# Output rows of six tiles from VectorE to ScalarE and GpSimd, squares to ScalarE, and a fourth slot between softmax and product with V, in a hybrid attention layer

## The chip, the core and the metric

The kernel runs on one core of one Trainium2 chip. Its engines work in parallel, each through its own list of instructions in order: PE (TensorE, matrix products), ACT (ScalarE), DVE (VectorE), POOL (GpSimd), and SP (SyncE), which here only issues transfers. PEld is PE's weight load. Semaphores make one engine wait for another. The metric is the device time of one execution in microseconds (us); the number given for a kernel is the median of several executions.

## The reference

One layer over 1024 tokens of 1024 columns. A joint projection feeds two groups of heads: group A is grouped-query attention with rotary positions, group B is attention over a neighbourhood of 8 x 16 tokens on a grid 64 wide. Both are gated, joined, projected, and added to x; a last RMSNorm follows.

```
h = _rmsnorm(x, norm_gain[l])
proj = h @ w_in[l]
q_a, k_a, v_a, g_a, q_b, k_b, v_b, g_b = jnp.split(proj, split_at, axis=-1)
... # RMSNorm and axial rotary positions of q_a and k_a
o_a = _gqa_blocked(q_a, k_a, v_a) * jax.nn.silu(g_a)
o_b = _neighbourhood_attn(q_b, k_b, v_b, na_rpb[l]) * jax.nn.silu(g_b)   # softmax(q k / 8 + bias) v, masked
mixed = jnp.concatenate([o_a, o_b], axis=-1)
x = x + mixed @ w_out[l]
return _rmsnorm(x, final_norm_gain)
```

The change bears on the neighbourhood attention (group B), on `mixed @ w_out`, and on the addition of x.

## The kernel before

The 1024 tokens are eight tiles of 128 rows (u = 0..7). Weights come in groups g of 256 columns: 0 to 12 are the joint projection, 13 to 16 the output projection. Each weight and each input of a projection is split into two fp16 numbers, a high part made by ACT (for weights L414, for a tile's mixed rows L933) and a low part made by DVE from the high one (L419, L937). A product of one tile with one group is 24 matmuls (eight chunks of the contraction by high-high, high-low, low-high), all recorded at line L504.

The span falls into four stages: projections (to about 160 us), attention A (160 to 360), attention B (364 to 506), and the rest of the output projections (506 to 549).

**Attention B** goes through 32 *pairs*: a tile u, taken in the order 0, 7, 1, 2, 3, 4, 5, 6, and two of its eight heads. For one pair PE makes the scores (L833, L836). DVE adds the bias and takes the row maximum (`b_qk`, L854, one instruction a head); ACT makes two exponentials (L856) and converts them to fp16 as the high part (L858); DVE makes the low part (`b_lo`, L863); a transposing transfer on SP's queue turns both (L865) into one of three buffers (`ptb`); PE multiplies them with V (L883 to L885). After every second pair DVE evacuates the product (L892 to L895) and POOL multiplies it into the gated rows `mixB` (L897).

**The mixed rows of a tile** are prepared for the output projection by `os_start`: the mean square (ACT the first half, L920; DVE the second, L925, which adds to the first), a scaling (L927), POOL's power -1/2 (L928), two high parts by ACT (L933), two low parts by DVE (L937), and two transposing transfers (L946).

**Output rows.** `out_gen` makes two products (256 columns each) into one PSUM bank, a *job*: of one tile and two groups, or of the first two tiles and one group. `add` on DVE then scales the rows and adds x, one instruction a product (L994), into a buffer loaded with x before. `fin_a` squares the finished half rows on ACT (L1019), and `fin_b` makes the last norm (L1025 to L1030).

**The order of the work.** `run_units` goes through slots i = 0, 1, ... In slot i the program is emitted in this order: some due jobs of ACT, the low part of pair i-1, the scores and softmax of pair i, more jobs of ACT, jobs of DVE, then 4.2 chunks (six matmuls each) of *filler* on PE, then the product with V of pair i-3 (`SKEW_B`). Filler is a queue of generators: gate projections (g = 11, 12) first, then output jobs. Work for ACT and DVE that isn't the softmax is put into a list with a cost (`job("dve", 0.5 * len(jobs), add, late=0)`), and `Flow.work` takes jobs from it in each slot until an allowance in microseconds is spent. So a change of costs or engines moves other jobs to other slots too. [...]

Of the kernel before, what the change touches and what calls it, by code (L numbers as in the profile page):

```python
# [8 lines left out]
F32 = mybir.dt.float32  # L9
F16 = mybir.dt.float16  # L10
BF16 = mybir.dt.bfloat16
AF = mybir.ActivationFunctionType
OP = mybir.AluOpType
# [3 lines left out]
P = 128  # L17
KC = 8
NU = 8
GC = 256  # L20
# [2 lines left out]
NX = 4  # L23
BASE_A, BASE_B = (1.72, 2.6, 2.8), (1.7, 1.6, 2.0)
HAND = 6
SKEW_A, SKEW_B = 5, 3
FILL_A = [(4, 5.0), (7, 4.2)]
FILL_A_END = 3.6
CHUNKS_A = 264
# [10 lines left out]
SLOTS = {"both": (16384, 2048, 4), "qc": (24576, 2048, 2), "stg1": (28672, 2048, 3), "stg": (18432, 2048, 3),  # L40
         "t": (0, 3072, 3), "ptb": (9216, 3072, 3), "th": (32896, 2048, 1), "y": (32896, 2048, 1),
         "p32": (AREA + 14464, 3072, 1)}
ORDER = (0, 7, 1, 2, 3, 4, 5, 6)
# [4 lines left out]
class Flow:  # L48
# [17 lines left out]
    def job(self, eng, cost, fn, *a, delay=1, late=1, key=None):  # L66

        self.jobs.append((late, self.slot + delay, self.number(), eng, cost, fn, a, key, self.tail))
# [83 lines left out]
def kernel(ctx: ExitStack, tc: tile.TileContext, x: bass.AP, w: bass.AP, wo: bass.AP,  # L152
# [3 lines left out]
    act, dve, pool, pe, sp = nc.scalar, nc.vector, nc.gpsimd, nc.tensor, nc.sync  # L156
# [3 lines left out]
    whl = ctx.enter_context(tc.tile_pool(name="whl", bufs=2))  # L160
# [7 lines left out]
    at, job = fl.at, fl.job  # L168
# [22 lines left out]
    def area(off, shape, dt):  # L191
        return carve(ar, off + 16384, shape, dt)

    turn = {}

    def slot(kind, shape, dt):

        off, size, n = SLOTS[kind]
        k = turn[kind] = turn.get(kind, -1) + 1
        off += k % n * size  # L200
        return area(off, shape[1:], dt) if off < AREA else carve(rq, off - AREA, shape[1:], dt)
# [13 lines left out]
    raw, wp, late, x2 = {}, {}, {}, {}  # L215
# [24 lines left out]
    for c in range(2):  # L240
        cs = slice(c * 512, (c + 1) * 512)
# [566 lines left out]
    def keys(u):  # L808

        a = max(u - 1, 0)  # L810
        return a, min(u + 1, NU - 1) - a + 1
# [49 lines left out]
    def b_lo(u, p):  # L861
        hl, p32 = hls.pop(("b", u, p))
        dve.scalar_tensor_tensor(hl[:, 1], p32, 2.0 ** 14, hl[:, 0], op0=OP.mult, op1=OP.subtract)  # L863
        pt = slot("ptb", [P, 4 * keys(u)[1], P], F16)
        sp.dma_start_transpose(pt, hl.rearrange("p a k -> p (a k)"))  # L865
        pts["b", u, p] = pt

    def b_pv(u, p):
        pt = pts.pop(("b", u, p))
        n = keys(u)[1]  # L870
        for e in range(2):
            b_pv_head(u, 2 * p + e, pt[:, e * n:e * n + n], pt[:, (2 + e) * n:(3 + e) * n])
# [29 lines left out]
    mT, rws, osp = {}, {}, {}  # L902
# [4 lines left out]
    def os_start(u):  # L907

        if not all({("b", u, c), ("a", u // 2, c * GC)} <= ready for c in range(2)):
            at(1, "post", os_start, u)  # L910
            return
        t = rws[u] = tn(f"os{u}", 4, "os")
        k = ORDER.index(u)
        hl = one.tile([P, 2, 1024], F16, tag=f"q{k % 2}0" if k > 3 else "gain", name=f"mhl{u}")
        osp[u] = [hl[:, 0], hl[:, 1]]
        ms = mixed(u)
        cs = [slice(i * 512, (i + 1) * 512) for i in range(2)]

        def sq():
            act.activation(late["r"][0][:, 2048:2560].bitcast(BF16), ms[0], AF.Square, accum_out=t[:, 0:1])  # L920
            job("dve", 0.95, scale, delay=0, late=0, key=("os", u))

        def scale():
            junk = late["r"][1][:, 2048:2560] if k else osp[u][0][:, cs[1]]
            dve.tensor_tensor_reduce(out=junk.bitcast(BF16), in0=ms[1], in1=ms[1], scale=1.0, scalar=t[:, 0:1],  # L925
                                     op0=OP.mult, op1=OP.add, accum_out=t[:, 1:2])
            dve.tensor_scalar(t[:, 1:2], t[:, 1:2], 2.0 ** -30, 1e-36, op0=OP.mult, op1=OP.add)  # L927
            pool.tensor_tensor(t[:, 2:3], t[:, 1:2], mh[:, :1], op=OP.pow)  # L928
            for i in range(2):
                job("act", 0.72, hi, i, delay=1, late=0, key=("os", u))  # L930

        def hi(i):
            act.activation(osp[u][0][:, cs[i]], ms[i], AF.Copy, scale=t[:, 2:3])  # L933
            job("dve", 0.8, lo, i, delay=0, late=0, key=("os", u))

        def lo(i):
            dve.scalar_tensor_tensor(osp[u][1][:, cs[i]], ms[i], t[:, 2:3], osp[u][0][:, cs[i]], op0=OP.mult, op1=OP.subtract)  # L937
            if i:
                dve.reciprocal(t[:, 3:4], t[:, 2:3])
                os_c(u)  # L940
        job("act", 0.82, sq, delay=1, late=0, key=("os", u))

    def os_c(u):
        mT[u] = [m.bitcast(F16).rearrange("p (a b) -> p a b", b=P) for m in mixed(u)]
# [36 lines left out]
    def load_x2(u):  # L981
        if u not in loaded:
            loaded.add(u)
            sp.dma_start(x2[u], rows_of(x, u, 1024, 0, 1024))

    def out_gen(jobs, done=()):

        pt = proj_tile(f"po{jobs[0][0]}_{jobs[0][1]}")
        rw = tn(f"rw{jobs[0][0]}_{jobs[0][1]}", 2, "rw")
        def add():  # L990
            for i, (u, g) in enumerate(jobs):
                cs = slice((g - 13) * GC, (g - 12) * GC)
                load_x2(u)
                dve.scalar_tensor_tensor(x2[u][:, cs], pt[:, i], rw[:, i:i + 1], x2[u][:, cs], op0=OP.mult, op1=OP.add)  # L994
        def then():
            job("dve", 0.5 * len(jobs), add, late=0)
            for u, h in done:
                job("act", 0.82, fin_a, u, h, delay=2, late=2)

        for i, (u, g) in enumerate(jobs):  # L1000
            need_w(g)
            fl.need(("os", u), lambda: u in mT)
            if i == 0 and jobs[-1] == (u, g + 1) and g + 1 in ready:
                dve.tensor_tensor(rw, col(RC + g, 2), rws[u][:, 3:4].to_broadcast([P, 2]), op=OP.mult)
            elif i == 0 or not both:
                dve.tensor_tensor(rw[:, i:i + 1], rws[u][:, 3:4], col(RC + g), op=OP.mult)
            both = i == 0 and jobs[-1] == (u, g + 1) and g + 1 in ready
            hi, lo = wp[g]
            seq = [(mT[u][a][:, k], b[:, k]) for k in range(KC) for a, b in ((0, hi), (0, lo), (1, hi))]
            yield from chunks([((pt[:, i], l, r), dict(start=n == 0, stop=n == 23))  # L1010
                               for n, (l, r) in enumerate(seq)], 6, then if i == len(jobs) - 1 else None)
# [185 lines left out]
    a, b = ORDER[2:4]  # L1197
# [7 lines left out]
    def hooks2(i):  # L1205
        hooks(i)
        for u, k in zip(ORDER, SPLIT_AT):
            if i - SKEW_B == k:
                at(0, "post", os_start, u)

    for u in ORDER[4:7]:
# [3 lines left out]
    def parts_b(i, back):  # L1215
        def first():
            if 1 <= i <= 32:
                b_lo(*ub[i - 1])
            if i < 32:
                b_qk(*ub[i])  # L1220
        return first, None, (lambda: b_pv(*ub[i - back])) if i >= back else None

    with run_units(32, SKEW_B, parts_b, rates(FILL_B, FILL_B_END), hooks2):
        pass
# [93 lines left out]
```

## Time and profile before

| | us |
|---|---|
| median of 3 runs (lowest to highest) | 556.71 (555.53 to 557.19) |
| the profiled execution's own time | 558.52 |
| its span, first to last instruction | 556.7 |
| PE busy (92% of the span) | 511.8 |
| DVE busy (81%) | 448.4 |
| ACT busy (67%) | 373.5 |
| POOL busy (29%) | 162.4 |
| mean granted clock of TensorE | 0.981 of full speed |

Rows of a timeline or of the chain of waits begin with the start in us and the duration in us; then come the engine, the line of the program, the operation, and output <- input by the names of the program. In a bracket stands how long the engine sat idle before, and for whom it waited. Rows of groups give the count (x), the total busy time and the mean duration in ns, and then the idle time before them and what ended it. `ar`, `rq` and `rest` are large buffers that are carved into many uses; `whl` is a split weight, `mhl` the split mixed rows, `x2b` the rows of x, `pjb` and `sb` are PSUM banks, `os` and `rw` hold row factors. Durations of instructions in a row overlap a little, so a distance between starts is shorter than the duration shown.

### The profile page before, as it was taken

The page shows a single profiled execution, that of the slowest core. Times are in us where ns is not written, and L with a number is a line of the kernel's source. Part 1 is how long each engine was busy: PE and PEld are TensorE (multiplying, and loading weights), DVE is VectorE, ACT ScalarE, POOL GpSimd, SP SyncE. Part 2 cuts the span into 40 slices and gives each one's busy share as a digit, 9 for nine tenths or more (in the row PEclk, how much of TensorE's full clock was granted, in tenths as well). Part 3 has the DMA queues.
Part 4 walks back from the last instruction along what each step waited for, and adds up shares of the span by engine and source line. Part 5 has one row for each costly group of instructions (what it writes and reads, how often), then busy time and mean ns, then how long its engine had stood idle before and what let it go on. Part 6 is the DMA issues. An engine that isn't in the chain of part 4 may idle for free.

```text
span 556.7 us, 12839 instructions
## 1 busy us (share of the span) xinstructions
PE 511.8 (92%) x5071; PEld 398.3 (72%) x5071; DVE 448.4 (81%) x911; ACT 373.5 (67%) x647; POOL 162.4 (29%) x185
## 2 busy tenths in 40 slices
PE   2667989989999999999999999999999989899994
PEld 0456878777887555568888888988777867688883
DVE  4599689789987988879879898777988988988532
ACT  5546465967887878787696796558688769662211
POOL 2385888571010000101001022633622211214000
PEclk9979999998999999999999999999999989999998
DMA  8998738779999999999997989644797999988612
GB/s 245 213 193 228 132 58 209 116 143 179 209 195 206 199 218 188 202 194 174 201 212 165 185 178 211 98 124 113 118 202 119 161 238 233 179 142 181 180 40 75
DMA packets 244509, 95.40 MB, mean 171 GB/s; under 512 B 235489, under 2 KB 236001, under 8 KB 242530
## 3 DMA queue, kind: packets, MB, share of 16 engines
q1 hardware_dynamic: 242434, 81.23, 78.3%
q0 software_dynamic: 1728, 12.58, 7.3%
q10 hardware_dynamic: 288, 0.79, 0.5%
q8 instruction: 39, 0.64, 0.5%
q14 instruction: 20, 0.16, 0.1%
HBM read 29.56 MB, written 4.19 MB: 61 GB/s over the span
## 4 chain that ended last, share of the span: by engine, by line
PE 52%; DVE 9%; ACT 6%; DMA 4%; issue 4%; POOL 1%; SPq 0%; DVEq 0%; POOLq 0%; ACTq 0%
PE pj L504 18%; PE pjb L504 8%; PE kb L504 7%; PE pv L775 5%; PE s L741 4%; PE s L743 4%; ACT rq L856 3%; PE pv L776 2%; DVE ar L854 2%; ACT ar L858 2%; PE sb L504 2%; DMA pt<-ar 2%; DMA x2b<-in_x_dram 1%; DVE ar L863 1%; DMA ar<-ar 1%
## 5 line engine op out<-in xcount | busy, mean ns | idle before, releaser
L504 PEld LDWEIGHTS <-hT 128*128 128x128 f16 x2112 | 204.3, 99 | 57.7 <-issue 16.0
L504 PE MATMUL pj<-whl,hT 128*128 128x256 f16 x1680 | 202.2, 279 | 20.2 <-DMA hT<-ar 7.5
L752 ACT ACTIVATE ar<-s,nm,sm 128x1024 f32<-128x1024 f32 x64 | 77.0, 1203 | 48.3 <-DVE nm L748 47.1
L748 DVE CUSTOM_DVE_ANT_0 ar<-s,sm 128x1024 bf16<-128x1024 f32 x64 | 81.9, 1280 | 30.1 <-PE s L743 28.4
L504 PEld LDWEIGHTS <-ar 128*128 128x128 f16 x768 | 74.5, 99 | 15.6 <-issue 4.5
L758 DVE TENSOR_TENSOR ar<-ar 128x1024 f16<-128x1024 f32 x64 | 79.1, 1237 | 1.4 <-ACT ar L753 1.3
L753 ACT ACTIVATE ar<-ar 128x1024 f16<-128x1024 f32 x64 | 67.6, 1057 | 2.3 <-DVE ar L758 0.4
L504 PE MATMUL pjb<-whl,ar 128*128 128x256 f16 x480 | 57.9, 277 | 3.1 <-DVE x2b L994 2.1
L856 ACT ACTIVATE rq<-ar,nm 128x384 f32<-128x384 f32 (+1 forms) x64 | 34.2, 580 | 32.8 <-DVE nm L854 32.1
L504 PE MATMUL pjb<-whl,hT 128*128 128x256 f16 x432 | 50.4, 273 | 0.1
L504 PE MATMUL kb<-hT,whl 128*128 128x512 f16 x192 | 44.5, 379 | 0.0
L784 POOL TENSOR_TENSOR ar<-ar,sum 128x256 f32<-128x256 f32 x16 | 11.4, 710 | 111.6 <-DVE ar L783 96.3
L419 DVE SCALAR_TENSOR_TENSOR whl<-raw,sm,whl 128x512 f16<-128x512 f32 x52 | 40.1, 798 | 2.8 <-ACT whl L414 2.8
L741 PE MATMUL s<-kTa,rq 128*128 128x512 f16 x128 | 38.5, 383 | 0.9 <-ACT ar L752 0.9
L775 PE MATMUL pv<-va,ar 128*128 128x128 f16 x384 | 39.3, 220 | 0.0
L775 PEld LDWEIGHTS <-ar 128*128 128x128 f16 x384 | 34.1, 98 | 5.5 <-issue 0.3
L776 PE MATMUL pv<-va,ar 128*128 128x64 f16 x384 | 38.0, 193 | 0.0
L897 POOL TENSOR_TENSOR ar<-ar,qkg 128x256 f32<-128x256 f32 x16 | 18.6, 1159 | 64.5 <-DVE qkg L895 63.2
L776 PEld LDWEIGHTS <-ar 128*128 128x128 f16 x384 | 33.4, 98 | 5.5 <-issue 0.3
L863 DVE SCALAR_TENSOR_TENSOR ar<-rq,ar 128x768 f16<-128x768 f32 (+1 forms) x32 | 30.5, 954 | 7.4 <-ACT ar L858 7.2
L414 ACT ACTIVATE whl<-raw,sm 128x512 f16<-128x512 f32 x52 | 34.0, 709 | 1.4 <-POOL sm L391 1.4
L391 POOL TENSOR_TENSOR sm<-wss,mh 128x1 f32<-128x1 f32 x17 | 10.5, 619 | 74.0 <-DVE wss L390 74.0
(165 smaller groups left out, 892.0 us busy)
## 6 DMA issues: line engine op xcount, KB each, us to landing
raw<-in_w_dram POOLq DMA_DIRECT2D x11, 1024.0 KB, 7.6
ar<-in_x_dram SPq DMA_DIRECT2D x7, 512.0 KB, 6.3
raw<-in_wo_dram SPq DMA_DIRECT2D x3, 1024.0 KB, 6.6
khh<-ar SPq DMA_DIRECT2D x16, 128.0 KB, 2.5
x2b<-in_x_dram SPq DMA_DIRECT2D x4, 512.0 KB, 6.9
x<-in_x_dram SPq DMA_DIRECT2D x4, 512.0 KB, 5.4
out_dram<-x2b SPq DMA_DIRECT2D x8, 256.0 KB, 3.7
out_dram<-x SPq DMA_DIRECT2D x7, 256.0 KB, 2.9
```

The costliest lines, as they stand in the source:

```text
L414: act.activation(wp[g][0][:, q], raw[g][:, q], AF.Copy, scale=col(S_ + g))
L419: dve.scalar_tensor_tensor(wp[g][1][:, q], raw[g][:, q], col(S_ + g), wp[g][0][:, q], op0=OP.mult, op1=OP.subtract)
L504: pe.matmul(*o[0], **o[1])
L741: pe.matmul(s[:, c * 512:(c + 1) * 512], q, kTa[:, 4 * c:4 * c + 4, hh], start=True, stop=False)
L748: dve.tensor_tensor_reduce(out=hl[:, 1].bitcast(BF16), in0=s, in1=col(SHA).to_broadcast([P, 1024]), scale=col(NSA), scalar=3e38, op0=OP.ad ...
L752: act.activation(p32, s, AF.Exp, bias=nm, scale=col(SCA), accum_out=rsum[hh, u][:, h:h + 1])
L753: at(0, "mid", lambda: act.activation(hl[:, 0], p32, AF.Copy))
L758: dve.tensor_tensor(hl[:, 1], p32, hl[:, 0], op=OP.subtract)
L775: pe.matmul(o, pt[:, kt], va[:, kt, hh], start=kt == 0, stop=False)
L776: pe.matmul(o[:, :D], pt[:, 8 + kt], va[:, kt, hh, :D], start=False, stop=kt == 7)
L856: act.activation(p32[:, e], t[:, e], AF.Exp, bias=nm, scale=-1.0)
L863: dve.scalar_tensor_tensor(hl[:, 1], p32, 2.0 ** 14, hl[:, 0], op0=OP.mult, op1=OP.subtract)
```

## The change

1. **Products with V later.** `SKEW_B` goes from 3 to 4 with `LATER = 17`: up to emission slot 16 the product with V still stands three slots behind; slot 17 has none; from slot 18 it stands four behind. So there is one slot more at the end. The ring of transposed probabilities gets a fourth buffer from pair 17 on, in a weight buffer that is free by then (`pt4`).
2. **Output rows.** Jobs of the first six tiles in the order (12 jobs, 24 products) are scaled out of PSUM by ACT (`put`, L1012) into a double buffer `ov`, which lies in the same weight buffer, and POOL adds them to x (L1018). The jobs of the last two tiles stay with DVE's `add`.
3. **Squares.** Both halves of a tile's mixed rows are squared by ACT (L934); DVE adds the two sums (L938).

```diff
-SKEW_A, SKEW_B = 5, 3
+SKEW_A, SKEW_B, LATER = 5, 4, 17
...
     def b_lo(u, p):
...
-        pt = slot("ptb", [P, 4 * keys(u)[1], P], F16)
+        shape = [P, 4 * keys(u)[1], P]
+        if ub.index((u, p)) >= LATER and "pt4" not in late:
+            late["pt4"] = whl.tile([P, 2, KC, GC], F16, tag="whl", name="pt4").rearrange("p a k c -> p (a k c)")
+            late["ov"] = late["pt4"][:, 2048:].bitcast(F32).rearrange("p (k a c) -> p k a c", k=2, a=2)
+            late["ring"] = [(LATER + k) % 3 for k in range(3)]
+            late["ring"].insert(0, 3)
+        if "ring" in late:
+            k = late["ring"][0]
+            late["ring"] = late["ring"][1:] + [k]
+            n = shape[1] * P
+            pt = (late["pt4"][:, :n].rearrange("p (a b) -> p a b", b=P) if k == 3 else
+                  area(SLOTS["ptb"][0] + k * SLOTS["ptb"][1], shape[1:], F16))
+        else:
+            pt = slot("ptb", shape, F16)
         sp.dma_start_transpose(pt, hl.rearrange("p a k -> p (a k)"))
...
         def sq():
-            act.activation(late["r"][0][:, 2048:2560].bitcast(BF16), ms[0], AF.Square, accum_out=t[:, 0:1])
-            job("dve", 0.95, scale, delay=0, late=0, key=("os", u))
+            for i in range(2):
+                act.activation(late["r"][0][:, 2048:2560].bitcast(BF16), ms[i], AF.Square, accum_out=t[:, i:i + 1])
+            job("dve", 0.3, scale, delay=0, late=0, key=("os", u))
 
         def scale():
-            junk = late["r"][1][:, 2048:2560] if k else osp[u][0][:, cs[1]]
-            dve.tensor_tensor_reduce(out=junk.bitcast(BF16), in0=ms[1], in1=ms[1], scale=1.0, scalar=t[:, 0:1],
-                                     op0=OP.mult, op1=OP.add, accum_out=t[:, 1:2])
+            dve.tensor_tensor(t[:, 1:2], t[:, 0:1], t[:, 1:2], op=OP.add)
...
-        job("act", 0.82, sq, delay=1, late=0, key=("os", u))
+        job("act", 1.6, sq, delay=1, late=0, key=("os", u))
...
+        def put():
+            k = turn["ov"] = turn.get("ov", -1) + 1
+            o = late["ov"][:, k % 2]
+            for i in range(2):
+                act.activation(o[:, i], pt[:, i], AF.Copy, scale=rw[:, i:i + 1])
+            (u, g), (v, _) = jobs
+            for i, n in ((0, 2),) if u == v else ((0, 1), (1, 1)):
+                w = jobs[i][0]
+                cs = slice((g - 13) * GC, (g - 13 + n) * GC)
+                load_x2(w)
+                pool.tensor_tensor(x2[w][:, cs], x2[w][:, cs], o[:, i:i + n].rearrange("p a c -> p (a c)"), op=OP.add)
+
         def then():
-            job("dve", 0.5 * len(jobs), add, late=0)
+            if "ov" in late and jobs[0][0] in ORDER[:6]:
+                job("act", 0.4 * len(jobs), put, late=0)
+            else:
+                job("dve", 0.5 * len(jobs), add, late=0)
...
-            if i - SKEW_B == k:
+            if i - 3 == k:
                 at(0, "post", os_start, u)
...
-        return first, None, (lambda: b_pv(*ub[i - back])) if i >= back else None
+        j = i - back + (i < LATER)
+        return first, None, (lambda: b_pv(*ub[j])) if j >= 0 and i != LATER else None
```

The change moves many rows of every engine. DVE between the maximum of pair 16 (the first four rows, `nm` 0 and 1) and its low part (L863), before:

```order
L854 ISA ar,nm_0_5584<-sb_4614,ar,sm 128x384
L854 ISA nm_0_5584 128x1
L854 ISA ar,nm_1_5587<-sb_4615,ar,sm 128x384
L854 ISA nm_1_5587 128x1
L925 ISA rest_4605,os_5530<-ar,os_5530 128x512
L925 ISA os_5530 128x1
L927 TENSOR_SCALAR os_5530<-os_5530 128x1
L419 SCALAR_TENSOR_TENSOR whl_5532<-raw_4930,sm,whl_5532 128x512 x2
L863 SCALAR_TENSOR_TENSOR ar<-rq,ar 128x768
```

and with the change:

```order
L854 ISA ar,nm_0_5585<-sb_4614,ar,sm 128x384
L854 ISA nm_0_5585 128x1
L854 ISA ar,nm_1_5588<-sb_4615,ar,sm 128x384
L854 ISA nm_1_5588 128x1
L938 TENSOR_TENSOR os_5532<-os_5532 128x1
L939 TENSOR_SCALAR os_5532<-os_5532 128x1
L419 SCALAR_TENSOR_TENSOR whl_5534<-raw_4930,sm,whl_5534 128x512 x3
L863 SCALAR_TENSOR_TENSOR ar<-rq,ar 128x768
```

The square became a small sum, and one more low part of a weight stands before the pair's own low part.

ACT around pairs 21 and 22 (`nm` 2 and 3 are pair 21's maxima, 4 and 5 pair 22's) and then around pairs 25 to 27, with the change:

```order
L856 ACTIVATE rq<-ar,nm_2_5909 128x384
L856 ACTIVATE rq<-ar,nm_3_5912 128x384
L858 ACTIVATE ar<-rq 128x768
L1012 ACTIVATE pt_5697<-pjb_4700,rw_13_5777 128x256 x2
L414 ACTIVATE whl_5841<-raw_5171,sm 128x512 x3
L945 ACTIVATE mhl_5855<-ar,os_5854 128x512 x2
L856 ACTIVATE rq<-ar,nm_4_5981 128x384
```

```order
L856 ACTIVATE rq<-ar,nm_3_6197 128x384
L858 ACTIVATE ar<-rq 128x768
L1012 ACTIVATE pt_5697<-pjb_4700,rw_13_6017 128x256 x2
L945 ACTIVATE mhl_6133<-ar,os_6132 128x512 x2
L856 ACTIVATE rq<-ar,nm_4_6264 128x384
L856 ACTIVATE rq<-ar,nm_5_6267 128x384
L858 ACTIVATE ar<-rq 128x768
L1047 ACTIVATE ar,of_6271<-x2b 128x512
L1012 ACTIVATE pt_5697<-pjb_4699,rw_15_6152 128x256 x2
L414 ACTIVATE whl_5841<-raw_5756,sm 128x512
L856 ACTIVATE rq<-ar,nm_6_6338 128x384
```

Before, there was no L1012; the three high parts of weights and the two of a tile that stand here behind pair 21 stood behind pair 20 (the names `whl` and `mhl` differ in their numbers):

```order
L856 ACTIVATE rq<-ar,nm_1_5868 128x384
L858 ACTIVATE ar<-rq 128x768
L414 ACTIVATE whl_5804<-raw_5171,sm 128x512 x3
L933 ACTIVATE mhl_5803<-ar,os_5802 128x512 x2
L856 ACTIVATE rq<-ar,nm_2_5933 128x384
```

POOL in the same stretch with the change (L910 is the product into `mixB`, L940 a tile's power):

```order
L910 TENSOR_TENSOR ar<-ar,qkg 128x256
L1018 TENSOR_TENSOR x2b<-x2b,pt_5697 128x256 x2
L940 TENSOR_TENSOR os_5854<-os_5854,mh 128x1
L910 TENSOR_TENSOR ar<-ar,qkg 128x256
L1018 TENSOR_TENSOR x2b<-x2b,pt_5697 128x256 x2
L910 TENSOR_TENSOR ar<-ar,qkg 128x256
L1018 TENSOR_TENSOR x2b<-x2b,pt_5697 128x512
L940 TENSOR_TENSOR os_6132<-os_6132,mh 128x1
```

Before, the powers (L928) stood directly behind the products into `mixB` (L897); now an addition of x stands between.

## The prediction

> **What bounds the kernel now.** I first read the busy time of each engine by stage (microseconds; PE, PEld, DVE, ACT, POOL in this order, then the granted clock, the DMA share and GB/s):
>
> ```profile
> core 0: us, PE busy (x) PEld busy (x) DVE busy (x) ACT busy (x) POOL busy (x), PEclk, DMA share, GB/s
> 364.00:437.00 73.00, 71.02 (x784) 56.91 (x783) 64.19 (x159) 56.80 (x111) 28.01 (x27) 1.00 0.68 125
> 437.00:506.00 69.00, 63.31 (x736) 50.21 (x735) 60.15 (x164) 48.39 (x92) 12.96 (x14) 0.98 1.01 197
> 506.00:549.00 43.00, 42.49 (x402) 37.90 (x400) 23.57 (x65) 7.65 (x20) 6.65 (x9) 1.00 0.45 121
> ```
>
> The change acts almost only in the second stage, the latter half of the neighbourhood attention, where PE is idle for 69.0 - 63.3 = 5.7 us and DVE for 8.9. Behind it PE runs the tail nearly without a gap. So the end moves with the moment at which the last softmaxes let PE go. Next the waits of that stage, PE's and then ACT's (total, times, longest):
>
> ```profile
> PE pjb L504 <- DVE x2b L994: 2.4, 3, 1.7
> PE pvb L883 <- DMA ar<-ar: 2.3, 2, 1.8
> ```
> ```profile
> ACT rq L856 <- DVE nm L854: 17.3, 11, 4.3
> ```
>
> The change is aimed at the first two rows: the additions L994 that free PE's banks late, and transposed probabilities that come late for the product with V. The question is what stands behind them. The chain of waits answers (start, duration, work):
>
> ```profile
> 479.95 0.87 DVE ar L863
> 480.82 0.53 DVE ar L854
> 481.45 0.50 ACT rq L856
> 481.97 0.61 ACT rq L856
> 482.60 0.84 ACT ar L858
> 483.44 0.62 ACT rest L920 x2
> 484.35 0.61 DVE ar L854
> ...
> 497.10 0.61 DVE ar L854
> ...
> 502.45 0.55 POOL os L928
> ...
> 505.03 0.80 DVE x2b L994 x2
> ...
> 540.76 9.50 issue
> ```
>
> This is a loop between DVE and ACT, one turn per pair of heads: bias and maximum (L854), two exponentials (L856), the convert (L858), the low part (L863), and only then the next pair's L854. The bare turn from 480.82 to 484.35 takes 3.53 us: 0.63 to the first exponential, 1.99 until the convert ends (481.45 to 483.44), 0.04, and 0.87 for the low part. Whatever the two rows hold between these that doesn't fit beside them is added. L854 of pair 16 starts at 429.50 (below), that of pair 31 at 497.10: 15 turns in 67.6 us, of which 15 x 3.53 = 53.0 are bare and 14.6 are extra.
>
> **The change, part by part.** Durations in that stage (count, busy us, mean ns):
>
> ```profile
> L419 DVE SCALAR_TENSOR_TENSOR whl<-raw,sm,whl 128x512 f16<-128x512 f32 x10 | 7.3, 744 | 1.6 <-ACT whl L414 1.6
> L937 DVE SCALAR_TENSOR_TENSOR mhl<-ar,os,mhl 128x512 f16<-128x512 f32 x7 | 6.8, 1012 | 0.0
> L994 DVE SCALAR_TENSOR_TENSOR x2b<-pjb,rw,x2b 128x256 f32<-128x256 f32 x14 | 6.2, 476 | 0.8 <-DMA x2b<-in_x_dram 0.8
> ```
> ```profile
> 429.50 0.61 DVE L854 CUSTOM_DVE_ANT_0 ar<-sb,ar,sm 128x384 f32<-128x384 f32 x1
> 430.57 0.75 DVE L925 CUSTOM_DVE_ANT_0 rest<-ar,os 128x512 bf16<-128x512 f32 x1
> 431.44 1.40 DVE L419 SCALAR_TENSOR_TENSOR whl<-raw,sm,whl 128x512 f16<-128x512 f32 x2
> 433.63 0.61 DVE L854 CUSTOM_DVE_ANT_0 ar<-sb,ar,sm 128x384 f32<-128x384 f32 x1
> 437.77 0.69 DVE L712 SCALAR_TENSOR_TENSOR ar<-ar,pjb 128x512 f32<-128x512 f32 x1 [0.36 <-ACT ar L706]
> 439.31 0.61 DVE L854 CUSTOM_DVE_ANT_0 ar<-sb,rq,sm 128x384 f32<-128x384 f32 x1
> ```
> ```profile
> 431.37 0.84 ACT L858 ACTIVATE ar<-rq 128x768 f16<-128x768 f32 x1
> 432.12 1.32 ACT L414 ACTIVATE whl<-raw,sm 128x512 f16<-128x512 f32 x2
> ```
>
> *Removed from DVE:* 24 additions of 0.48 us and eight squares of 0.75, less eight small sums of about 0.15; in the five turns between pairs 21 and 30 that held two additions (0.8 per couple), and the four that held a square, this is 5 x 0.8 + 4 x 0.6 = 6.4 us. It pays only where DVE came last in a turn.
>
> *Added to ACT:* two scaled copies per job (the put) and a second square per tile. No 128x256 copy from PSUM is in this trace. Its bounds are an exponential of that width out of SBUF and a 128x512 operation out of PSUM:
>
> ```profile
> L856 ACT ACTIVATE rq<-ar,nm 128x256 f32<-128x256 f32 x16 | 7.2, 500 | 7.5 <-DVE nm L854 6.8 <-ACT ar L706 0.6
> L706 ACT ACTIVATE ar<-pjb,sm 128x512 f32<-128x512 f32 x9 | 6.0, 670 | 0.0
> ```
>
> Pipelined behind each other I take 0.42 each (0.35 to 0.6), 0.85 for a put. A square is 0.62 (L920 in the chain) and 0.1 to read its sum.
>
> *Added to POOL:* the addition of x. Bounds are L897 (128x256, two inputs) and L717 (128x512):
>
> ```profile
> 444.98 0.73 POOL L897 TENSOR_TENSOR ar<-ar,qkg 128x256 f32<-128x256 f32 x1 [4.96 <-DVE qkg L895]
> 455.70 1.16 POOL L897 TENSOR_TENSOR ar<-ar,qkg 128x256 f32<-128x256 f32 x1 [6.03 <-DVE qkg L895]
> ```
> ```profile
> L717 POOL TENSOR_TENSOR ar<-ar 128x512 f32<-128x512 f32 x3 | 4.5, 1498 | 1.2 <-DVE ar L716 1.1
> ```
>
> I take 1.3 for 512 columns, range 1.2 to 2.3. POOL has 56 us free of 69, so the time itself is hidden; its place is not. The tile's power (L928 before) now stands behind this addition, the addition behind the put, and the tile's high parts on ACT behind the power.
>
> *Moved:* the four-slot skew draws gate and output products forward, and the rows of ACT and DVE fall anew. This is what costs. Turn by turn, extra over the bare 3.53, with 2.65 (0.63 + 1.99 and a step between) from L854 to the convert's end:
>
> - Pair 16: ACT makes three high parts of weights after the convert, of which one stood ahead of it before; DVE's three low parts wait for the last. 2.65 + 3 x 0.65 + 0.75 + 0.87 = 6.2, extra 2.7 (before 433.63 - 429.50 = 4.13, extra 0.6).
> - Pair 17: its rows are unchanged (evacuation, two L937, a gate): 439.31 - 433.63 = 5.68, extra 2.1.
> - Pair 21: a put and three high parts after the convert, then the low part: 2.65 + 0.85 + 1.95 + 0.75 + 0.87 = 7.1, extra 3.5.
> - Pair 22: the rows of pair 17 less the gate (0.69 and its wait of 0.36), extra 1.1.
> - Pairs 24 and 25: four squares on ACT behind the convert of pair 23 take 4 x 0.72 = 2.9, and 1.5 is free until the next exponential is due (3.53 + 0.63 - 2.65): extra 1.3; with three more squares behind pair 24, another 0.6.
> - Pairs 26 and 30: put, addition, power (0.55, L928 in the chain) and two high parts (1.32 as the couple at 432.12), all ahead of the exponentials: 0.85 + 1.3 + 0.55 + 1.32 = 4.0 where 1.5 is free: extra 2.5 each.
> - Pair 27: four low parts behind three high parts that come after the convert, which is itself 0.6 late: extra 3.2.
> - The remaining six turns lose their additions, squares or low parts and are bare: 0.
>
> Sum 2.7 + 2.1 + 3.5 + 1.1 + 1.3 + 0.6 + 5.0 + 3.2 = 19.5, against 14.6: +4.9. Ahead of pair 16 the second square waits on ACT for POOL's product (before, DVE's L925 waited so) and gates wait for a tanh moved behind the convert: +0.7 (0 to 0.9).
>
> *Products with V four slots behind:* this removes the 2.3 us of PE's waits for transposes. I cost it at nothing, since PE then waits for the same softmaxes at its scores or banks; one more product, 0.6, stands behind the last. PE's two shorter waits of the first row (0.7 together) may vanish: -0.1 in all. The fourth buffer adds no transfer. DVE's wait for a load of x (0.8 in the row of L994) would be POOL's, with the power behind it.
>
> So the end moves by 4.9 + 0.7 - 0.1 = +5.5. The profiled execution took 558.5, so 564.0; that is 1.8 over the median of the runs shown, 556.71, from which the same step gives **562.2**. The tail's work and its 8 us of drain (in the last chain row) stay.
>
> By the Trainium skill's "GPSIMD Engine Reference", section 4, "When to use GPSIMD", such additions belong on VectorE, and its specifications say that GpSimd's SBUF access collides with VectorE instructions that read two SBUF inputs. The trace agrees on the collision: 0.73 us alone, 1.16 beside L937. From its ratio of 1.96 between the two engines one would estimate 0.93 us for an addition that takes DVE 0.48, within the bounds taken; the sum would not change by more than 0.6.
>
> **Rivals.** *Faster, DVE was the bound.* For it: a couple of additions stands in the chain to the very end (505.03), and ACT waits 17.3 us for L854, room for all that it is given (eight puts of 0.85 and four squares of 0.72 in that stage: 9.7). If the new rows of ACT fitted there, of the 6.4 us between the 0.8 that the chain shows at 505.03 and all would come off, say 4.3, two thirds: 552.4. All of PE's idle time in the two stages, 5.7 + 2.0, is the floor, 549. Against: ACT's waits lie before the exponentials, and the new rows stand between a convert and them, with waits of their own.
>
> *The same, gains and losses cancel.* If POOL's additions don't hold the powers (the put comes early enough, or the tile's sums late enough), pairs 26 and 30 are bare, -5.0: 557.2. For it: the power's own wait for DVE's sums isn't known. Against: the put is the first of ACT's rows behind the convert, so the addition can't start before it.
>
> *Slower still, POOL and DVE collide.* Sixteen additions run beside two-input rows of DVE. If half of them lengthen a DVE row on the loop by the 0.43 seen above, that is 3.4 more: 565.6. And PE's new gaps can halve its clock, as here:
>
> ```profile
> 450.00:453.00 3.00, 1.24 (x25) 0.70 (x22) 2.56 (x6) 2.56 (x5) 0.00 (x0) 1.00 0.67 141
> 453.00:457.00 4.00, 4.00 (x23) 2.73 (x23) 3.17 (x9) 1.76 (x3) 1.16 (x1) 0.57 1.12 237
> ```
>
> After 1.76 us of idle PE ran at 0.57 for 4 us, 1.7 us lost; before, the loop hid that. In the last slots it would not: 567. The Trainium skill's "TensorE: Matmul & The Clock Gate", Part 1, has a free-running window of about 3.4 us, so that a gap may or may not be hit.
>
> *Not done as said:* if the planner fell back to DVE for the outputs, the time would be near 557; the order of rows speaks against it.
>
> **How the numbers follow.** Forecast 0.47, its own range 559 to 566 (the six copies in pairs 21, 26 and 30 at both bounds, -0.4 to +1.1; the two additions, -0.2 to +2.0; up to 2.5 less where one late row hides another). Collision 0.13; same 0.14; faster 0.26. Times agree to about 0.3% (1.7 us), so slower is over 558.4 and faster under 555.0: slower 0.47 + 0.13 = 0.60. The range reaches down to the faster case's 552 and up to the collision's 567.
>
> **What would show it.** Right: L854 of pair 31 starts some 5 us later after pair 16 of the same program; ACT's high parts of tiles wait for POOL's power for 2 us in pairs 25 and 29; DVE waits for L414 in pairs 16, 21 and 27 for over 1 us each; PE's waits for transposes vanish while its waits for banks (now freed by ACT) or for DVE grow. Wrong: turns of pairs 21 to 30 near 3.6 to 4.2 us, DVE with fewer waits, and PE's idle time under 3 us there. A single mis-sized step, the power behind the addition, would take back 5.0 us.

## The result and the profile after

The changed kernel took 563.64 us (median of 4 runs, 561.90 to 564.59) against 556.95 (median of 4, 555.53 to 557.88). The ratio is 1.0089, with a 95% interval of 1.0059 to 1.0118: slower by about 5 us (3 to 7). The medians lie further apart, by 6.7 us; which of the two is nearer can't be told from four runs each. The forecast was 562.2, a step of 5.5. The profiled execution took 563.15 with a span of 561.4.

The busy time by stage, in the columns of the table shown before (PE, PEld, DVE, ACT, POOL):

```profile
364.00:437.00 73.00, 70.44 (x771) 56.13 (x768) 60.59 (x151) 57.37 (x113) 26.04 (x26) 1.00 0.64 118
437.00:512.00 75.00, 63.90 (x730) 51.32 (x730) 53.83 (x146) 55.94 (x114) 20.64 (x26) 0.95 0.96 185
512.00:555.00 43.00, 41.41 (x406) 36.99 (x403) 22.69 (x55) 14.14 (x36) 12.48 (x15) 1.00 0.44 117
```

The change did what it says: in the latter half of attention B, DVE is busy for 53.8 us where it was 60.2, ACT for 55.9 where it was 48.4, POOL for 20.6 where it was 13.0. But the stage takes 75 us instead of 69, and PE is idle in it for 11.1 us instead of 5.7. DVE got lighter and waits more. The waits from 430 to 516 us, of PE, DVE and ACT in turn:

```profile
PE pjb L504 <- ACT pt L1012: 9.3, 3, 4.8
PE pjb L504 <- DMA ar<-ar: 1.6, 1, 1.6
...
DVE ar L863 <- ACT ar L858: 11.5, 11, 1.7
DVE whl L419 <- ACT whl L414: 6.1, 3, 2.7
DVE ar L854 <- DMA ar<-ar: 2.0, 1, 2.0
...
ACT mhl L945 <- POOL os L940: 6.1, 4, 1.9
```

PE's waits of 2.3 us for the transposes of a pair, in front of products with V, are gone, and so are those for DVE's additions. In their place PE waits 9.3 us for a bank that ACT's copy (L1012) frees late. Behind that stands DVE, which waits for ACT's converts and high parts, and ACT, which waits for POOL's power. In its first two rows DVE waits 17.6 us; in the kernel before (430 to 510 us) the same two rows came to 4.8:

```profile
DVE ar L863 <- ACT ar L858: 3.2, 4, 1.5
DVE whl L419 <- ACT whl L414: 1.6, 2, 0.9
```

The places of the prediction, first DVE at pair 16 (start, duration, in brackets the idle time before):

```profile
428.29 0.60 DVE L854 CUSTOM_DVE_ANT_0 ar<-sb,ar,sm 128x384 f32<-128x384 f32 x1
...
431.62 2.08 DVE L419 SCALAR_TENSOR_TENSOR whl<-raw,sm,whl 128x512 f16<-128x512 f32 x3 [1.91 <-ACT whl L414]
...
434.48 0.61 DVE L854 CUSTOM_DVE_ANT_0 ar<-sb,ar,sm 128x384 f32<-128x384 f32 x1
```

The turn takes 434.48 - 428.29 = 6.19 us instead of 4.13: DVE stands for 1.91 us before the high parts that ACT makes behind the convert. Its rows come in the order of the list shown with the change. Then DVE at pairs 20 and 21:

```profile
449.75 0.96 DVE L863 SCALAR_TENSOR_TENSOR ar<-rq,ar 128x768 f16<-128x768 f32 x1 [0.70 <-ACT ar L858]
452.75 0.62 DVE L854 CUSTOM_DVE_ANT_0 ar<-sb,ar,sm 128x384 f32<-128x384 f32 x1 [2.05 <-DMA ar<-ar]
...
456.88 2.28 DVE L419 SCALAR_TENSOR_TENSOR whl<-raw,sm,whl 128x512 f16<-128x512 f32 x3 [2.71 <-ACT whl L414]
...
460.02 0.60 DVE L854 CUSTOM_DVE_ANT_0 ar<-sb,rq,sm 128x384 f32<-128x384 f32 x1
```

Pair 21's turn takes 7.27 us; ahead of it stands a wait of 2.05 us that the prediction did not have. Last ACT, and below it POOL, between pairs 25 and 26:

```profile
475.67 0.84 ACT L858 ACTIVATE ar<-rq 128x768 f16<-128x768 f32 x1
476.42 0.82 ACT L1012 ACTIVATE pt<-pjb,rw 128x256 f32<-128x256 f32 x2
479.17 1.33 ACT L945 ACTIVATE mhl<-ar,os 128x512 f16<-128x512 f32 x2 [1.93 <-POOL os L940]
480.41 1.10 ACT L856 ACTIVATE rq<-ar,nm 128x384 f32<-128x384 f32 x2
```
```profile
477.32 1.31 POOL L1018 TENSOR_TENSOR x2b<-x2b,pt 128x512 f32<-128x512 f32 x1 [5.65 <-ACT pt L1012]
478.59 0.54 POOL L940 TENSOR_TENSOR os<-os,mh 128x1 f32<-128x1 f32 x1
```

Read in order: the put ends at 477.24, POOL's addition waits for it and takes 1.31, the power 0.54 behind it, and only then can ACT make the tile's high parts; the exponentials of pair 26 stand behind these in ACT's list and start at 480.41, although their maxima were begun at 477.49. That is the chain of five steps that the prediction had worked out, at nearly the prices that it took.

### The profile page after: what moved, and what is told of

It reads as the page before. It is cut to its first block, busy times and chain, and to the rows that moved or that the text cites. A ratio compares the mean times of both kernels' runs of the same rounds, so it can differ in the third digit from the quotient of the medians.

```text
span 561.4 us, 12873 instructions
## 1 busy us (share of the span) xinstructions
PE 511.4 (91%) x5071; PEld 399.1 (71%) x5071; DVE 438.1 (78%) x879; ACT 387.6 (69%) x687; POOL 175.5 (31%) x201
## 4 chain that ended last, share of the span: by engine, by line
PE 49%; DVE 10%; ACT 8%; issue 5%; DMA 5%; POOL 0%; DVEq 0%; POOLq 0%; ACTq 0%
PE pj L504 17%; PE kb L504 7%; PE pjb L504 7%; PE pv L775 4%; PE s L741 4%; PE s L743 4%; DMA ar<-ar 4%; ACT rq L856 3%; ACT ar L858 2%; PE pv L776 2%; DVE ar L854 2%; PE sb L504 2%; DVE whl L419 2%; DVE ar L863 2%; DMA pt<-ar 2%
## 5 line engine op out<-in xcount | busy, mean ns | idle before, releaser
L753 ACT ACTIVATE ar<-ar 128x1024 f16<-128x1024 f32 x64 | 67.6, 1056 | 3.3 <-DVE ar L758 1.4
L504 PE MATMUL pjb<-whl,ar 128*128 128x256 f16 x480 | 56.1, 273 | 1.7 <-ACT pt L1012 1.7
L863 DVE SCALAR_TENSOR_TENSOR ar<-rq,ar 128x768 f16<-128x768 f32 (+1 forms) x32 | 30.4, 951 | 15.6 <-ACT ar L858 15.3
L414 ACT ACTIVATE whl<-raw,sm 128x512 f16<-128x512 f32 x52 | 34.0, 709 | 1.4 <-POOL sm L391 1.4
L910 POOL TENSOR_TENSOR ar<-ar,qkg 128x256 f32<-128x256 f32 x16 | 15.3, 958 | 55.3 <-DVE qkg L908 37.1
```

The costliest lines, as they stand in the source:

```text
L414: act.activation(wp[g][0][:, q], raw[g][:, q], AF.Copy, scale=col(S_ + g))
L504: pe.matmul(*o[0], **o[1])
L753: at(0, "mid", lambda: act.activation(hl[:, 0], p32, AF.Copy))
```

## The experiments

The kernels were timed in groups, each group on one chip and beside the kernel before; so kernels of different groups are best compared by their ratios to it. "Turn" is the distance between the starts of L854 of one pair and the next, read from each kernel's profile.

### Each part by itself

The kernel before with one part of the change. Only the squares:

```diff
-            act.activation(..., ms[0], AF.Square, accum_out=t[:, 0:1])
-            job("dve", 0.95, scale, delay=0, late=0, key=("os", u))
+            for i in range(2):
+                act.activation(..., ms[i], AF.Square, accum_out=t[:, i:i + 1])
+            job("dve", 0.3, scale, delay=0, late=0, key=("os", u))
...
-        job("act", 0.82, sq, delay=1, late=0, key=("os", u))
+        job("act", 1.6, sq, delay=1, late=0, key=("os", u))
```

> The kernel before with both squares of the mixed rows on ACT and nothing else of the change. My theory (what counts is where a row stands in the turn between DVE and ACT): the rows regroup so that the turns of pairs 10 and 14 wait for a gate behind a late tanh and pair 16 for a third high part, and turns 19 to 30 hardly move: from pair 8 to pair 31 some 0.9 us more than before, so 557.9 (556.5 to 559). Rival 1 (DVE is the bound): eight times 0.6 us less on DVE, 552 to 555. Rival 2 (the loss is in the outputs and POOL's additions alone): within 0.3 us of before.

Measured: 565.73, ratio 1.0150 (1.0125 to 1.0175), as slow as the whole change or more. Every stated case missed. The turns of pairs 10, 14 and 16 were late, as I had worked out (4.76, 4.76, 6.18), and from pair 8 to 31 they took 105.5 us instead of 102.8; but that is only 2.8 of some 8. The other part lies behind the last softmax, in the chain of waits:

```profile
506.74 1.41 DVE x2b L1029 x2
...
508.50 0.56 POOL of L1026
509.08 1.41 DVE x2b L1029 x2
...
511.40 4.45 PE pjb L504 x24
```

In this order DVE makes two final norms (L1029), each with a wait for POOL, ahead of the additions that free PE's banks. PE waits for them twice, 4.0 us together, and starts its next output product at 511.40. It takes 4.45 us for 24 matmuls that take 2.6 at the full clock, since its clock is halved after the wait (row of the windows, PE's busy time first, the clock behind POOL):

```profile
512.00:515.00 3.00, 3.00 (x17) 2.21 (x16) 3.00 (x15) 0.89 (x4) 1.37 (x2) 0.54 0.42 128
```

So the squares cost in two places, and by these rows it is in both what now stands ahead of what.

Only the skew and the fourth buffer:

```diff
-SKEW_A, SKEW_B = 5, 3
+SKEW_A, SKEW_B, LATER = 5, 4, 17
... # pt4, ring and j = i - back + (i < LATER) as in the change; add() and the squares as before
```

> The kernel before with the products with V four slots behind and the fourth buffer, outputs and squares on DVE as before. My theory: the rows regroup; the turns of pairs 16 to 20 stay, those of 21, 25 and 29 lose some 1.8 us each, those of 22, 24, 26 and 30 gain 0.5 to 1.2: from pair 8 to 31 2.1 us less than before, and 0.6 for one more product at the end: 555.2 (554 to 556.5). Rival (a quarter of the loss comes from each slot that the skew adds): 558 to 560. Rival (PE's waits for transposes were the bound): 554.4, with turns unchanged.

Measured: 555.99, ratio 0.9950 (0.9924 to 0.9977): faster than before by half a per cent, within my range. The turns from pair 8 to 31 took 99.6 us, 3.2 less than before.

Only the outputs (`put` on ACT, the addition on POOL), three slots and three buffers:

```diff
-SKEW_A, SKEW_B, LATER = 5, 4, 17
+SKEW_A, SKEW_B, LATER = 5, 3, 17
... # no fourth buffer in the ring, b_pv(*ub[i - back]) and the squares as before; put() as in the change
```

> The kernel before with the outputs of six tiles by ACT and POOL, products with V three behind, squares shared by ACT and DVE as before. My theory: the loss is not in the outputs by themselves; turns 21, 23, 25 and 29 lose the couples of additions, 24 and 27 gain 0.6 and 2.0 behind a put: 1.8 us less than before, 555.1 (554 to 556.5). Rival 1 (POOL and DVE collide, or ACT is over-full with the puts): 558.5 to 560. Rival 2 (additions were the bound): 551 to 553.

Measured: 557.49, ratio 0.9995 (0.9971 to 1.0019). No change; I had expected 1.8 us of gain, but the turns from 8 to 31 took 103.4, which is 0.7 more than before. Turns 21, 25 and 29 lost their couples of additions, 0.8 to 1.6 us each. But 23, which was to lose one too, rose from 4.76 to 6.83, and 30, which was to stay, by 1.15. In turn 23 DVE waited 3.1 us for transposes, the longest of this row,

```profile
DVE ar L854 <- DMA ar<-ar: 3.6, 2, 3.1
```

and such a wait my sum of instructions does not contain.

### The whole change less one part

The second square back on DVE, with its charges:

```diff
-            for i in range(2):
-                act.activation(..., ms[i], AF.Square, accum_out=t[:, i:i + 1])
-            job("dve", 0.3, scale, delay=0, late=0, key=("os", u))
+            act.activation(..., ms[0], AF.Square, accum_out=t[:, 0:1])
+            job("dve", 0.95, scale, delay=0, late=0, key=("os", u))
...
-        job("act", 1.6, sq, delay=1, late=0, key=("os", u))
+        job("act", 0.82, sq, delay=1, late=0, key=("os", u))
```

> The kernel after with the second square and its sum back on DVE: outputs by ACT and POOL, products with V four behind. My theory now (the squares bring most of the loss by regrouping the rows of ACT and of DVE): turns 10, 14 and 16 as in the kernel before, 21 at 3.7, 26 at 4.7, 27 at 6.3, 30 at 4.7; the sum from pair 8 to 31 is 0.4 us under that of before: 556 to 557.5. Rival 1 (puts and POOL's additions bear the loss): 560 to 563. Rival 2 (each part of the change adds by itself, and the two other parts alone were -2.0 and -0.5): 554.5 to 555.5.

Measured: 554.97, ratio 0.9955 (0.9928 to 0.9983). Faster than both kernels, and better than I had it: the number is that of the rival in which parts add, but the next two kernels refute adding. From pair 8 to 31 the turns take 101.1 us, and PE's waits for the put shrink from 9.3 to one:

```profile
PE pjb L504 <- ACT pt L1013: 1.7, 1, 1.7
```

The outputs back on DVE:

```diff
-            if "ov" in late and jobs[0][0] in ORDER[:6]:
-                job("act", 0.4 * len(jobs), put, late=0)
-            else:
-                job("dve", 0.5 * len(jobs), add, late=0)
+            job("dve", 0.5 * len(jobs), add, late=0)
```

> The kernel after with the outputs back on DVE: both squares on ACT, products with V four behind. My theory: turns 10, 14 and 16 as late as in the kernel after, 21 at 5.6, 23 and 24 at 4.2, 26 at 5.4; the sum from pair 8 to 31 equals that of before; additions no longer stand behind the last norms as with the squares alone: 556.5 to 559. Rival 1 (squares cost 8 us in any company): 562 to 565. Rival 2 (the outputs bring nothing and cost nothing): within 1 us of after.

Measured: 558.21, ratio 1.0018 (1.0000 to 1.0036), as forecast.

Three slots and three buffers again:

```diff
-SKEW_A, SKEW_B, LATER = 5, 4, 17
+SKEW_A, SKEW_B, LATER = 5, 3, 17
...
-            late["ring"] = [(LATER + k) % 3 for k in range(3)]
-            late["ring"].insert(0, 3)
...
-        j = i - back + (i < LATER)
-        return first, None, (lambda: b_pv(*ub[j])) if j >= 0 and i != LATER else None
+        return first, None, (lambda: b_pv(*ub[i - back])) if i >= back else None
```

> The kernel after with products with V three behind again (three buffers): both squares on ACT, outputs by ACT and POOL. My theory: turns 10, 14 and 16 late, 21 at 5.7 to 6.5, 24 and 25 at 4.8, 27 at 5.5, the sum from pair 8 to 31 about 1 to 3 us over before; PE waits for transposes again: 558 to 561. Rival (the skew brings the loss): 556 to 557. Rival (the squares cost 8 us in any company): 564 to 566.

Measured: 559.94, ratio 1.0033 (1.0015 to 1.0050), as forecast. The parts don't add: squares with the skew give +0.18%, with the outputs +0.33%, alone +1.5%. That the three parts alone sum to +0.95%, near the whole's +0.89%, is then chance.

### The power ahead of POOL's addition, and no additions

```diff
+    later_add = []
... # add_now() makes the additions that are kept in later_add
-                pool.tensor_tensor(x2[w][:, cs], x2[w][:, cs], o[:, i:i + n].rearrange("p a c -> p (a c)"), op=OP.add)
+                later_add.append((w, x2[w][:, cs], o[:, i:i + n].rearrange("p a c -> p (a c)")))
+            at(0, "end", add_now)
... # fin_a calls add_now(u) first
```

> The kernel after, with POOL's additions of x emitted at the end of their slot, so that a tile's power no longer stands behind an addition; the same instructions. My theory: turns 26 and 30 fall from 5.8 and 5.9 us to 4.7 each, 27 from 6.5 to about 6.3, 21 unchanged at 7.1: 2.5 to 3.0 us less than after, so about 560.9 (559.5 to 562). Rival 1 (the power behind the addition costs all of 5 us, as predicted): 558.6. Rival 2 (POOL's additions cost by colliding with DVE, wherever they stand): within 0.5 us of after, 563 to 564.

Measured: 561.99, ratio 1.0091 (1.0057 to 1.0125). Turns 26, 27 and 30 fell from 5.80, 6.50 and 5.88 to 4.70, 6.28 and 4.70. ACT now goes from the put to the high parts without a wait:

```profile
475.57 0.82 ACT L1019 ACTIVATE pt<-pjb,rw 128x256 f32<-128x256 f32 x2
476.29 1.33 ACT L945 ACTIVATE mhl<-ar,os 128x512 f16<-128x512 f32 x2
477.51 1.11 ACT L856 ACTIVATE rq<-ar,nm 128x384 f32<-128x384 f32 x2
```

The mechanism is confirmed in the turns; the end gained less. In the profiles it came 2.2 us earlier, of which 0.6 lie before pair 16. The medians differ by 1.7, but the ratios (1.0089 and 1.0091) not at all, so a gain in time is not shown. The reason for "less" is in PE's rows. In the kernel after, and in this one (a row of the chain):

```profile
496.87 2.13 PE L504 MATMUL pjb<-whl,ar 128*128 128x256 f16 x18 [1.65 <-ACT pt L1012]
```
```profile
494.70 2.12 PE pjb L504 x18
```

These matmuls wait for the put behind pair 29, and PE has no gap of 0.3 us after them until 512. So the end is set there, one turn before my sum ended, and what turn 30 costs or gains is hidden behind PE's work: with the power first, turn 30 is 1.2 us shorter, and the span left behind it 1.2 us longer (59.7 instead of 58.5).

```diff
-                pool.tensor_tensor(x2[w][:, cs], x2[w][:, cs], o[:, i:i + n].rearrange("p a c -> p (a c)"), op=OP.add)
```

> The kernel after without POOL's additions of the six tiles' outputs to x (their output rows are left out of the result, so the final norm sees x alone for these tiles). My theory: the additions cost by their place ahead of the powers, not by POOL's time or by colliding with DVE: turns 26 and 30 at 4.7, 27 at 6.3, as with the power ahead of the additions, so 561 to 562.3, within 0.8 us of that kernel. Rival 1 (collision of POOL with DVE's two-input rows): 558 to 559.5, with turn 22 at 4.7 where it is 5.24. Rival 2 (the additions cost nothing at all): 563 to 564.5.

In this kernel the additions are left out: the rows of six tiles lack the output projection. Measured: 561.58, ratio 1.0079 (1.0048 to 1.0110), not to be told from the power-first kernel's 1.0091. Turn 22 fell to 4.69, from 5.25, and 21 from 7.27 to 7.07; the turns from 8 to 31 sum to 106.1, with the power first to 106.9. So once they stand behind the power, POOL's additions cost the loop under 1 us in all, collisions with DVE included; what they cost above that in the kernel after, 2.5 us in turns 26, 27 and 30, was their place.

### Order or work

This pair asks whether the squares cost by ACT's time or by the order that their *charge* brings. The planner charges each job against an allowance per slot. First, all instructions of the change, but charged as before:

```diff
-            job("dve", 0.3, scale, delay=0, late=0, key=("os", u))
+            job("dve", 0.95, scale, delay=0, late=0, key=("os", u))
...
-        job("act", 1.6, sq, delay=1, late=0, key=("os", u))
+        job("act", 0.82, sq, delay=1, late=0, key=("os", u))
```

> The kernel after (all of the change), but the planner charges the squares and their sum as before the change: 0.82 for ACT and 0.95 for DVE in place of 1.6 and 0.3. The instructions are those of after; only the order is that of a kernel whose squares are shared. My theory (some two thirds of what the squares cost is the order that their charge brings, one third their time on ACT): the sum of turns from pair 8 to 31 is 3 us over the kernel with squares on DVE (101.1) and 4 to 5 us under after (109.8), turn 21 at 4.0 and 27 at 6.3: 557 to 559. Rival 1 (the squares' time on ACT is what costs): 562 to 564. Rival 2 (order alone): 554.5 to 555.5.

Measured: 557.51, ratio 0.9995 (0.9975 to 1.0014), and 103.7 us for the turns from 8 to 31: my own case, two thirds order and one third work, and neither rival. The whole change, with not one instruction less, is as fast as the kernel before in another order. At pair 16 DVE finds two low parts in place of three, and no wait:

```profile
430.10 0.61 DVE L854 CUSTOM_DVE_ANT_0 ar<-sb,ar,sm 128x384 f32<-128x384 f32 x1
...
431.43 1.40 DVE L419 SCALAR_TENSOR_TENSOR whl<-raw,sm,whl 128x512 f16<-128x512 f32 x2
...
434.04 0.61 DVE L854 CUSTOM_DVE_ANT_0 ar<-sb,ar,sm 128x384 f32<-128x384 f32 x1
```

Then the counterpart, the second square on DVE but charged 1.6 and 0.3:

> The counterpart: products with V four behind, outputs by ACT and POOL, the second square on DVE, so ACT has less to do than in the kernel after; but the planner charges 1.6 and 0.3 as if both squares were on ACT. My theory (order decides): turns 10, 14, 16, 21, 26, 27 and 30 as in the kernel after (4.8, 4.8, 6.2, 7.1, 5.9, 6.7, 5.9), sum from pair 8 to 31 within 1 us of after's 109.8 less 2 us for the wait for transposes where it doesn't come: 561 to 564. Rival 1 (the squares' time on ACT is what costs): 554.5 to 556.5. Rival 2 (half and half): 558 to 560.

Measured: 563.20, ratio 1.0100 (1.0077 to 1.0123). With less for ACT to do than in the kernel after, it is as slow. Turns 10, 14, 16, 21, 26, 27 and 30 are 4.8, 4.8, 6.2, 7.3, 5.8, 6.5 and 5.9, as forecast from the order alone. Pair 16 again:

```profile
429.24 0.60 DVE L854 CUSTOM_DVE_ANT_0 ar<-sb,ar,sm 128x384 f32<-128x384 f32 x1
...
432.55 2.08 DVE L419 SCALAR_TENSOR_TENSOR whl<-raw,sm,whl 128x512 f16<-128x512 f32 x3 [1.31 <-ACT whl L414]
...
435.42 0.61 DVE L854 CUSTOM_DVE_ANT_0 ar<-sb,ar,sm 128x384 f32<-128x384 f32 x1
```

The square fills 0.6 us of DVE's wait there, and the turn has the same 6.18 us. The four kernels side by side (median, ratio to before):

| | both squares on ACT | second square on DVE |
|---|---|---|
| charged 1.6 and 0.3 | 563.64, 1.0089 | 563.20, 1.0100 |
| charged 0.82 and 0.95 | 557.51, 0.9995 | 554.97, 0.9955 |

Down a column only the order differs: by 6 and 8 us in the medians, 5 and 8 by the ratios. Along a row the square moves. In the upper row that makes 0.4 us, which is within the noise. In the lower one it makes 2.5 us; the intervals there (0.9975 to 1.0014 and 0.9928 to 0.9983) hardly overlap, and the sums of turns differ by 2.6 us the same way (103.7 and 101.1), in 17, 25, 26 and 30 by 0.5 to 0.7 each. So most of what the squares cost is the order that their charge brings; the work itself costs little where a wait hides it, as at pair 16, and some 2 us where none does.

### A larger allowance for ACT

The kernel with the second square on DVE and its old charges, and one number more:

```diff
-BASE_A, BASE_B = (1.72, 2.6, 2.8), (1.7, 1.6, 2.0)
+BASE_A, BASE_B = (1.72, 2.6, 2.8), (1.7, 1.3, 2.0)
```

> Products with V four behind, outputs by ACT and POOL, squares shared as before, and the planner's allowance for ACT 0.3 us larger per slot (the second number of BASE_B 1.3 in place of 1.6). If order decides, a better one should beat both kernels: turn 27 falls from 6.3 to 4.2, 25 from 4.1 to 3.6, 24 and 26 rise by 0.7 each; 1.5 to 2 us less than with the old allowance: 553 to 554.5. Rival (PE, not the turns, now sets the end): 554.5 to 555.5. Rival (a larger share for ACT delays the exponentials): 556 to 558.

Measured: 555.08, ratio 0.9950 (0.9926 to 0.9974), the same as without it; the further 1.5 to 2 us that I had forecast did not come. Turn 27 fell to 4.97 and 25 to 3.62, but 20 rose to 6.42 (DVE waited 1.0 us for transposes before the next L854) and 24 to 5.13; the sum from pair 8 to 31 is 101.0, as before the edit. The time is that of the rival in which PE sets the end; but since the turns took as long as without the edit, this run doesn't decide for it. The three kernels that are faster than before (skew alone, and the change with the second square on DVE, with either allowance) stand at 555.0 to 556.0.

## Why the prediction was right, step by step

**The bound** was named rightly: the turn of DVE and ACT, not DVE's load and not PE's waits. DVE lost 6 us of work in the stage and the stage grew by 6. Three of the signs that the prediction named are there as it named them: ACT waits 1.93 us for POOL's power in pair 25 (and as long in pair 29), DVE waits over 1 us for L414 in pairs 16, 21 and 27, and PE's waits for banks grew in place of those for transposes.

**The turns.** The forecasts and what the profile after shows, in us:

| pair | 16 | 17 | 18, 19 | 20 | 21 | 22 | 23 | 24 | 25 | 26 | 27 | 28, 29 | 30 | sum |
|---|---|---|---|---|---|---|---|---|---|---|---|---|---|---|
| forecast | 6.2 | 5.7 | 3.5 each | 3.5 | 7.1 | 4.6 | 3.5 | 4.8 | 4.1 | 6.0 | 6.7 | 3.5 each | 6.0 | 72.5 |
| measured | 6.19 | 5.22 | 3.62, 3.69 | 5.74 | 7.27 | 5.25 | 3.61 | 4.62 | 3.99 | 5.80 | 6.50 | 3.62, 3.59 | 5.88 | 74.6 |

The measured sum ends at the maximum of pair 31,

```profile
502.88 0.61 DVE L854 CUSTOM_DVE_ANT_0 ar<-sb,rq,sm 128x384 f32<-128x384 f32 x1
```

502.88 - 428.29 = 74.6, against 67.6 before: +7.0 where +4.9 was forecast. Nearly all of the 2.1 is turn 20: DVE waits 2.05 us there for transposes, because the softmax of pair 21 writes into one of three buffers (`t`), out of which the transposes of pair 18 still read. So the term "the remaining six turns are bare" was wrong at pair 20. The fourth buffer of the change stands on the other side of the transpose and doesn't help there; "the fourth buffer adds no transfer" is true, but looked at the one side only. In the kernel before, this wait was 0.4 us in all.

**Ahead of pair 16** +0.7 was forecast, from the gates and the second square. From pair 8 to 16 both kernels take 35.2 us: turns 10 and 14 did lose 0.7 and 1.0, but 11 and 15 gave 0.3 and 1.0 back. The term was 0.

**The end.** -0.1 was forecast behind pair 31, and it was -1.1: the span has 58.5 us left from there, 59.6 before. The step that failed is taking the last softmax as the place that sets the end; it is the put behind pair 29. Of the two 2.5 us charged to pairs 26 and 30, the second lies beside PE's work. So three misses, +2.1, -0.7 and -1.0, nearly cancel, and the total is better than its parts; that much of it is luck. (The spans of the two profiles differ by 4.7 only, since that of the kernel before was already 1.2 us behind at pair 8, and 1.6 at pair 0, ahead of all that the change touches.) The last row of the chain, which the prediction gives as 8 us of drain, is 9.50 us long in both kernels and so doesn't enter the sum.

**The prices** held: a put's two copies take 0.82 (0.85 taken), POOL's addition 1.31 (1.3), the power 0.54 (0.55), two high parts 1.33 (1.32).

**The rivals.** "DVE was the bound" fell: its 6 us less went into waits. "Gains and losses cancel" by powers ahead of additions was wrong in its size: moving the powers gave 2.5 us in turns 26, 27 and 30, and in the time 1.7 us by the medians and none by the ratios, not 5.0, since turn 30 is off the path and turn 26 keeps the put and the high parts, 1.2 us above the bare turn. The collision of POOL and DVE, +3.4, was under 1 us. (The product on POOL that the prediction took as "alone", 0.73 us, ran beside DVE's L712, which has one of its inputs in PSUM.) PE's clock did halve behind the longest new gap, at 478 to 482, but PE waited again for ACT at 496.87, 1.65 us, so the halving set nothing; behind the gap at 453 it did not halve:

```profile
453.30:456.20 2.90, 0.14 (x2) 0.00 (x0) 0.84 (x6) 2.76 (x6) 0.32 (x1) 1.00 0.99 228
456.20:460.20 4.00, 3.98 (x48) 3.21 (x48) 3.31 (x6) 3.13 (x5) 2.04 (x3) 1.00 1.18 211
...
478.00:482.00 4.00, 4.00 (x32) 2.45 (x30) 3.10 (x11) 2.80 (x5) 2.34 (x4) 0.50 0.81 102
```

Here 2.8 us of idle cost no clock, in the kernel before 1.8 us did. By the Trainium skill's "TensorE: Matmul & The Clock Gate", Part 1, the clock falls after at least one idle window of about 3.4 us, and the window is free-running. The gap of 2.8 us agrees with that. The one of 1.8 us doesn't, since it is shorter than a window and the clock fell to 0.57 all the same; here the measurement decides, and what tells the two gaps apart stays open.

**What the prediction had wrong.** It gave the loss to where rows stand, which holds, but it said that the four-slot skew puts them there ("This is what costs"). The skew alone made the kernel 0.5% faster, and with three slots the rest of the change is still slower than before, though less so (1.0033). What puts them there is above all the charge of the squares, the smallest part, in company with the other two: in the planner 1.6 in place of 0.82 takes the allowance of a slot, a tanh and a high part go behind the convert, and later work follows. With the old charge and the second square on DVE the other two parts give 0.45% of gain, no more than the skew alone; the outputs bring nothing. So the forecast, which was read off the finished order of rows, could be near without the right cause of that order. Why the squares alone cost more than with the others is answered only for that kernel's end (final norms ahead of additions), not for every turn.

## What to carry to other kernels

Where two engines hand one chain back and forth, count what stands between the two hand-overs in each engine's list, turn by turn; busy time says little, and an engine relieved of 6 us can wait 12 more. A job moved to the engine that makes the next link costs its place as well as its time, and a producer on a third engine (here a power behind an addition behind a copy) adds every link of its own queue. In a kernel whose order comes from charged costs, changing a charge is itself a change: test it without the work, and the work without it.

## What the runs showed of the hardware beyond that

In the kernel after, the transposing transfers of pairs into the three old buffers took 3.7 us (median) from issue to landing between 385 and 437 us and 3.9 between 462 and 500, but 8.3 (median of three) between 438 and 462; the chain has

```profile
443.46 9.15 DMA ar<-ar
```

for pair 18, just the one that DVE waited for. Four loads of 512 KB and one of 1024 KB are issued in that stretch, from 441.55 to 454.93. Two transfers into the fourth buffer, issued at 440.06 and 460.24, ahead of the first load and behind the last, took 3.7. The kernel before has the same loads there and 7.5 us (median of five), though DVE hardly waited for them. That the loads cause it is argued from the time alone; no kernel without them was run, so it stays open.
